# The preparation of a pair of RWKV heads as three workers: front, values, back

## The chip, the cores and the metric

The kernel runs on one core of a Trainium2 chip. The metric is the device time of one execution in microseconds (us). The profile tells of five engines, each with its own queue of instructions: TensorE (PE, with its weight loads as PEld), VectorE (DVE), ScalarE (ACT), GpSimd (POOL) and SyncE (SP, which here only issues DMAs).

## What is computed

One decoder layer on 512 tokens of width 2048, in float32: a forgetting-attention branch (fox, 8 heads of 128) and an RWKV-7 branch (16 heads of 64), each with a gate, are projected, gated by sigmoids, added, multiplied by `w_out`, added to the input and normalized. Cut to the RWKV branch, which the change concerns:

```python
h = _rmsnorm(x, norm_gain)
u = h @ w_in
...
r, kr, vr, z_b, w_down, a_down = _split(_token_shift(u_rwkv, mix), RWKV_SIZES)
w = -softplus(-(w0 + tanh(w_down) @ w2)) - 0.5
decay = exp(-exp(w));  a = sigmoid(a0 + a_down @ a2)
kk = heads(kr * k_k) / norm;  kr = kr * (1 + (a - 1) * k_a)
for t in tokens:                      # per head, S is 64 x 64
    sa = S @ (-kk[t])
    S = S * decay[t] + outer(sa, (kk * a)[t]) + outer(v[t], kr[t])
    y[t] = S @ r[t]
o_b = (groupnorm(y) * ln_w + ln_b + bonus) * silu(z_b)
```

## The kernel before, in words

**Tiles of the big products.** The input is normalized and transposed once (`hhi`, `hlo`: a high and a low part, so that each float32 product is three matmuls of 512 columns). A *tile* `u_<name>` is 128 output columns of `w_in`: 16 blocks of the contraction by three matmuls, 48 in all. Its weights come in four *pieces* of 256 KB: `load_raw` (L237) issues a load on SP into one of `RAWS` buffers, ScalarE makes the high part `whi` (L262), VectorE the low part `wlo` (L263). `next_piece` (L240) issues loads `RAWS` pieces ahead and emits the two splits three pieces ahead of use.

**Order of the tiles.** `units` (L295) lists them: pair 0, pair 1, then a fox head and a pair by turns, at last fox head 6. A pair of RWKV heads has four tiles in the order k, r, z, v; a fox head has q, k, v, z. After them (`stage1`, L859 on) come the merge tiles `u_g` (three of them, then fox head 7, then one g tile and one projection `p` by turns) and the output product `o`. The first `p` needs the results of all eight pairs, loaded back from memory (`oraw`, L870).

**Workers and the planner's clock.** The order of TensorE's and of SP's instructions is the order in which the program emits them (`manual_schedule`, L152); VectorE, ScalarE and GpSimd are ordered by the framework from the program order and priorities. The small steps are generators (*workers*) that yield a lag. `clock` advances with each matmul by its planned cost (`mm`, L125: 512/2370 us for one of a tile); after each matmul of a tile `drive` (L112) runs every worker whose lag has passed, first worker in the list first. So a lag says how much TensorE work is put between two steps. The lags stand in `LAG` (L51).

**A pair's preparation before** (`rwkv_prep`, L489), a single worker that starts when the one of the pair before is done (`after=[prep, chain2]`, L851):
- front: the small `lora` weights are loaded and split (L498 to L502), the square of k is split; after a lag of 3.57 (`in`) the products `kn`, `lw` and `la` (eight matmuls); from them on VectorE, ScalarE and GpSimd the decay (scan, exponentials E1 and E2), `kp`, the normalized `kk` (reciprocals, L535), `AR` (L540, L541), `BK` (four products on 64 partitions, L546 and L549), `rkk` and its split `rhi`, `rlo`;
- values: after 11.25 (`vt0`), and when the v tile is there (`vin`), transposes of v (`vt`), the bonus (`bn`, L574), centring of `SV`, copies to `AV` (L586, on GpSimd);
- back: after 9.77 (`sc0`) the scores `sc` (two halves of 16 recorded matmuls each, 8.02 apart) from `BK` and `AR`, masked into `G`; `G` goes through memory and comes back as `Lt` (L609, L613); the solve, 31 steps of a product and a reduction on VectorE (L618 to L621); 42 after its emission the result goes through memory again (L626 to L634); after 5.04 (`inv`), and when the chain before is done, `bt`, `gp` and `dp`.

**The chain** (`rwkv_chain`, L673) runs the state over eight chunks (`z`, `sa`, `st`), then `y`, the group norm and the store to `ob_d`. Chain and preparation of different pairs overlap. **Fox heads** (`fox_head`, L751) are workers too, last in the list.

Buffers that the change touches: `EK` holds E2 and `kp` and later `Lt`; `W` and `Wt` hold `lora` and `lora_l` and later the solve; four tags (`t0`, `a`, `t2`, `EK`) are used again by the first merge tiles, which is why `stage1` waits for `free["rw"] == 7` (L859), set when the solve of the last pair is emitted (L622).

Of the kernel before, what the change touches and what calls it, by code (L numbers as in the profile page):

```python
# [9 lines left out]
F32 = mybir.dt.float32  # L10
F32R = mybir.dt.float32r
# [12 lines left out]
CH = 64  # L24
NC = T // CH
LORA = 96
# [19 lines left out]
AHEAD = 8  # L46
SQ2 = 6
SQ3 = 14
RAWS = 5

LAG = {"in": 3.57, "vt0": 11.25, "vt": 1.47, "sc0": 9.77, "sc": 8.02, "bt": 1.78, "inv": 5.04, "sub": 42.0, "gp": 2.84, "ch": 1.31, "z": 1.2, "sa": 1.6, "st": 2.01, "gn": 3.3, "gv": 1.42, "f0": 4.37, "f1": 2.11, "f2": 11.56, "f3": 3.14, "f4": 4.67, "f5": 16.0, "f6": 1.12}  # L51


@with_exitstack
def hybrid_layer(
# [23 lines left out]
    clock = [0.0]  # L79

    class Worker:
        def __init__(self, gen, after):
            self.gen, self.after, self.ready, self.done = gen, after, clock[0], False

        def runnable(self):
            return not self.done and all(w is None or w.done for w in self.after)
# [6 lines left out]

    workers = []

    def spawn(gen, after=(), first=True):
        w = Worker(gen, after)
        workers.insert(0, w) if first else workers.append(w)
        return w

    def step_one(force=False):
# [19 lines left out]
    def until(cond):  # L121
        while not cond():
            yield "wait"
# [360 lines left out]
    hs = [slice(0, 64), slice(64, 128)]  # L484
    free = {}

    made, zs = {}, {}

    def rwkv_prep(p, r, k):  # L489
        def w(tag, shape=(P, T), n=None, bufs=1, dt=F32):  # L490
            return (keep if tag in KEEP else rw).tile(list(shape), dt, tag=tag, name=f"{n or tag}_{p}", bufs=bufs)

        def col(base):
            return par[:, base + p:base + p + 1]

        v = vT[:, CH:CH + T]
        E1, DT = E1s[p % 2], DTs[p % 2]
        lora = w("W", (LORA, 2, P), n="lora")  # L498
        nc.sync.dma_start(lora[:, 0, :], rwkv_w2[0][:, p * P:(p + 1) * P])
        nc.sync.dma_start(lora[:, 1, :], rwkv_a2[0][:, p * P:(p + 1) * P])  # L500
        lo2 = [w("lora", (LORA, 2, P), dt=F32R, n="lora_h"), w("Wt", (LORA, 2, P), dt=F32R, n="lora_l")]
        split(*lo2, lora)  # L502
        ksq = w("t2", n="ksq")
        S.activation(ksq, k, AF.Square, scale=col(R_KK))
# [34 lines left out]
        AR = w("AR", (P, NC, 2 * CH), bufs=2)  # L539
        V.scalar_tensor_tensor(AR[:, :, 0:CH], c3(kk), -1.0, E1[:, :, 0:CH], ALU.mult, ALU.mult)  # L540
        tt(V, AR[:, :, CH:], c3(r), E1[:, :, 1:CH + 1])  # L541
        BK = w("BK", (P, NC, 2 * CH))
        tt(G, kk, kk, a)
        for q in range(2):
            h = hs[q]
            tt(V, BK[h, :, 64 - 64 * q:128 - 64 * q], c3(kp)[h], c3(E2)[h])  # L546
        for q in range(2):
            h = hs[q]
            tt(V, BK[h, :, 64 * q:64 * q + 64], c3(kk)[h], c3(E2)[h])  # L549

        t2 = w("t2", n="rkk")
        V.scalar_tensor_tensor(t2, r, col(R_RK), kp, ALU.mult, ALU.mult)
        rhi, rlo = w("t0", n="rhi", dt=F32R), w("t3", n="rlo", dt=F32R)
        split(rhi, rlo, t2)
        free["rk"] = p
        yield LAG["vt0"]
        while free.get("vin", -1) < p:
            yield 1.0

        SV, AV = w("SV", (P, NC, 2, CH), bufs=2), w("AV", (P, NC, 2, CH), bufs=2)  # L560
        for w0 in (0, 4, 8):
            ps = ps_ms(f"vt_{p}_{w0}").rearrange("p (c t) -> p c t", c=4)
            n = min(4, 9 - w0)
# [16 lines left out]
        for q in range(2):  # L580
            h = hs[1 - q]
            vm = w(f"vm{q}", (P, NC))
            V.tensor_reduce(vm[h], SV[h, :, q, :], AX.X, ALU.add)
            V.scalar_tensor_tensor(SV[h, :, q, :], vm[h].unsqueeze(2).broadcast_to([64, NC, CH]), -1.0 / 64,
                                   SV[h, :, q, :], ALU.mult, ALU.add)
            G.tensor_copy(AV[h, :, q, :], SV[h, :, q, :])  # L586
            G.memset(SV[hs[q], 0, q, :], 0.0)
        yield LAG["sc0"]
        while free.get("chain", -1) < p - 2:
            yield 1.0  # L590

        Gm = w("G", (P, NC, 2, 2, CH), bufs=2)
        mask4 = smask.rearrange("p (k t) -> p k t", k=2)[:, None].broadcast_to([P, 4, 2, CH])
# [12 lines left out]
        for q in range(2):  # L606
            for b in range(2):
                o = 64 * q + 32 * b
                nc.sync.dma_start(l_d[16 * q + 8 * b:16 * q + 8 * b + 8].rearrange("c s t -> s c t"),  # L609
                                  Gm[o:o + 32, :, 0, q, 32 * b:32 * b + 32])  # L610
        Lt = w("EK", (P, 32, 32), n="Lt")
        for g in range(4):
            nc.sync.dma_start(Lt[32 * g:32 * g + 32], l_d)  # L613
        V.memset(Lt.rearrange("p s t -> p (s t)")[:, 0:1024:33], 1.0)
# [3 lines left out]
        for i in range(1, 32):  # L618
            tt(V, tmp[:, :, 0:i + 1], W[:, :, 0:i + 1],
               Lt[:, 0:i + 1, i].unsqueeze(1).broadcast_to([P, 8, i + 1]))  # L620
            V.tensor_reduce(W[:, :, i], tmp[:, :, 0:i + 1], AX.X, ALU.add)  # L621
        free["rw"] = p  # L622
        yield LAG["sub"]
        w_d = dram.tile([32, 4, 256], F32, tag="w_d", bufs=2, name=f"w_d_{p}")
        for g in range(4):
# [41 lines left out]
        for q in range(2):  # L667
            h = slice(64 * q, 64 * q + 32)
            (V.tensor_copy if q else S.copy)(DT[h, :, 64 * q + 32:64 * q + 64], dp[h, 0:NC, :])
            S.copy(Gm[hs[q], :, 0, q, :], AR[hs[q], :, 0:CH])  # L670
        made[p] = (AR, BT, DT, SV, AV, Gm, E1, bonus)

    def rwkv_chain(p):  # L673
        def w(tag, shape=(P, T), n=None, bufs=1, dt=F32):
            return (keep if tag in KEEP else rw).tile(list(shape), dt, tag=tag, name=f"{n or tag}_{p}", bufs=bufs)

        def col(base):
            return par[:, base + p:base + p + 1]

        AR, BT, DT, SV, AV, Gm, E1, bonus = made.pop(p)  # L680
        yield LAG["ch"]


        for c in range(NC):
            with tc.high_priority(offset=HP):
                zp = ps_ch(f"z_{p}_{c}")
                mm(zp, Gm[:, c, 0].rearrange("p q t -> p (q t)"), SV[:, c])
                zt = w("zt", (P, CH), bufs=2)
                V.tensor_copy(zt[hs[0]], zp[hs[0], 0, :])
                S.copy(zt[hs[1]], zp[hs[1], 1, :])  # L690
                pre = w("pre", (P, CH))
                if c < NC - 1:
                    for q in range(2):
                        S.activation(pre[hs[q]], SV[hs[q], c, q, :], AF.Copy, scale=E1[hs[q], c, CH:CH + 1])
            yield LAG["z"]
            with tc.high_priority(offset=HP):
                sa = ps_ch(f"sa_{p}_{c}")
                mm(sa[:, 0, :], DT[:, c, :], zt)
                V.tensor_copy(AV[hs[0], c, 0, :], sa[hs[0], 0, :])
                S.copy(AV[hs[1], c, 1, :], sa[hs[1], 0, :])  # L700
            yield LAG["sa"]
            if c < NC - 1:
                with tc.high_priority(offset=HP):
                    st = ps_ch(f"st_{p}_{c}")
                    mm(st, BT[:, c, :], AV[:, c])
                    for q in range(2):
                        V.scalar_tensor_tensor(SV[hs[q], c + 1, q, :], st[hs[q], q, :], E1[hs[q], c, CH:CH + 1],
                                               pre[hs[q]], ALU.mult, ALU.add)
                yield LAG["st"]

        y = psm.tile([P, NC, CH], F32, tag="y", bufs=1, name=f"y_{p}")
        for c in range(NC):
            for q in range(2):
                mm(y[hs[q], c, :], SV[hs[q], c, q, :], AR[hs[q], c, CH:], start=(c == 0), stop=False,
                   skip_group_check=True)
        for c in range(NC):
            for q in range(2):
                mm(y[hs[q], c, :], AV[:, c, q, :], Gm[:, c, 1, q, :], start=False, stop=(c == NC - 1),
                   skip_group_check=True)
        yield LAG["st"]  # L720
        free["chain"] = p

        z = zs.pop(p)
        with tc.high_priority(offset=HV):
            yf = y.rearrange("p c t -> p (c t)")
            ysq = ps_ms(f"ysq_{p}")
            S.activation(ysq, yf, AF.Square)
            yhi, ylo = w("y", n="yhi", dt=F32R), w("y2", n="ylo", dt=F32R)
# [82 lines left out]
    def fox_unit(i):  # L811
# [13 lines left out]
        def run(i=i, ins=ins):  # L825
            yield from fox_head(i, ins)
            free["fox"] = i
        spawn(run(), first=False)

    def stage1():  # L830
        ps = yield from u_tile("ad")
        ad = keep.tile([LORA, T], F32, tag="t2", name="ad")
        shift(ad, ps, R_MUA, LORA)
        split(*ads, ad)
        prep = chain = chain2 = None
        ins = {}
        for kind, i in units:
            if kind == "rw":
                for nm, blk in (("k", 1), ("r", 0), ("z", 3), ("v", 2)):
# [8 lines left out]
                        ins[nm] = dst  # L848
                    shift(dst, ps, R_MU + blk * 8 + i)
                    if nm == "r":  # L850
                        prep = spawn(rwkv_prep(i, ins["r"], ins["k"]), after=[prep, chain2])  # L851
                        chain2 = chain
                        chain = spawn(rwkv_chain(i), after=[prep, chain])
                    if nm == "z":
                        zs[i] = dst
                free["vin"] = i
            else:
                yield from fox_unit(i)
        yield from until(lambda: free.get("rw", -1) == 7)  # L859


        mg_stack = ExitStack()
# [172 lines left out]
```

## Time and profile before

| | |
|---|---|
| median of 3 runs | 1706.83 us (1701.46 to 1707.15) |
| the profiled execution | 1702.85 us |
| its span, first to last instruction | 1701.1 us, mean granted clock 0.991 |
| TensorE matmul busy | 1640.5 us (96%), 8506 instructions |
| VectorE busy | 962.1 us (57%) |
| ScalarE busy | 716.9 us (42%) |
| GpSimd busy | 91.1 us (5%) |
| chain that ended last | 85% TensorE, 9% VectorE, 2% ScalarE, 1% DMA |

Matmuls are pipelined: the recorded duration of one (0.39 us for 512 columns) is longer than the distance of their starts (10.88 us for 48, that is 0.227), so a short wait can hide in the busy time, and distances of starts tell more than durations. Engines are named as in the profile, and L133 is line 133 of the kernel. A float32 product of small tiles is recorded as two instructions.

### The profile page before, as it was taken

To read this page: it belongs to the slowest core of one execution; us is meant where nothing else is said; L and a number is where in the kernel's file an instruction comes from. 1 tells how busy PE (TensorE), PEld (TensorE's weight loads), DVE (VectorE), ACT (ScalarE), POOL (GpSimd) and SP (SyncE) were. 2 spreads that over 40 slices of the span, in tenths; PEclk is the share of its full clock that TensorE was granted. 3 is DMA by queue.
4 is the path that set the end of the run, shared out by engine and by line. 5 is a ranking of instruction groups with operands and counts; after the bars stand their busy time and mean duration, and the time that the engine had idled before them with its cause. 6 is when DMAs were issued, how large, how long until landed. Compare 5 with 4: busy or idle time off the path is not lost.

```text
span 1701.1 us, 23407 instructions
## 1 busy us (share of the span) xinstructions
PE 1640.5 (96%) x8506; PEld 1332.3 (78%) x8506; DVE 962.1 (57%) x2005; ACT 716.9 (42%) x1455; POOL 91.1 (5%) x149
## 2 busy tenths in 40 slices
PE   6999999999999999999999988999999999999998
PEld 6878778788787787787877876888888888888886
DVE  6657577876786677867877644223233333353432
ACT  7522653654635536555355344222223222243322
POOL 3000000100001001000010000000000000001110
PEclk9999999999999999999999998999999999999999
DMA  5334234333333333333333324335334333343422
GB/s 170 84 90 107 71 100 105 77 97 97 82 91 84 83 97 83 97 85 90 88 90 90 96 63 130 99 95 147 95 97 145 97 96 97 98 141 137 133 81 99
DMA packets 287977, 170.23 MB, mean 100 GB/s; under 512 B 38790, under 2 KB 270830, under 8 KB 287222
## 3 DMA queue, kind: packets, MB, share of 16 engines
q1 hardware_dynamic: 284358, 156.13, 34.5%
q0 software_dynamic: 2064, 9.46, 1.6%
q10 hardware_dynamic: 1440, 3.15, 0.5%
q8 instruction: 67, 1.10, 0.3%
q14 instruction: 48, 0.39, 0.1%
HBM read 158.19 MB, written 10.50 MB: 99 GB/s over the span
## 4 chain that ended last, share of the span: by engine, by line
PE 85%; DVE 9%; ACT 2%; DMA 1%; issue 1%; SPq 1%; ACTq 0%; POOL 0%; DVEq 0%
PE u_g L133 21%; PE o L133 10%; PE p L133 10%; PE u_fk L133 5%; PE u_fq L133 5%; PE u_v L133 5%; PE u_z L133 5%; PE u_r L133 5%; PE u_fv L133 4%; PE u_fz L133 3%; PE u_k L133 3%; DVE BK L478 2%; DVE kn L535 1%; PE fo L133 1%; PE y L133 1%
## 5 line engine op out<-in xcount | busy, mean ns | idle before, releaser
L133 PE MATMUL u_g<-hhi,whi_g 128*128 128x512 f32 x512 | 200.7, 392 | 0.0
L133 PE MATMUL u_g<-hhi,wlo_g 128*128 128x512 f32 x512 | 200.5, 392 | 0.0
L133 PE MATMUL u_g<-hlo,whi_g 128*128 128x512 f32 x512 | 199.8, 390 | 0.0
L263 DVE TENSOR_TENSOR wlo_g<-raw_g,whi_g 128x512 fp32r<-128x512 f32 x128 | 88.5, 692 | 170.7 <-ACT whi_g L262 163.1
L262 ACT ACTIVATE whi_g<-raw_g 128x512 fp32r<-128x512 f32 x128 | 80.7, 632 | 223.6 <-PE u_g L133 120.6
L133 PEld LDWEIGHTS u_g<-hhi,wlo_g 128*128 128x128 f32 x512 | 96.3, 188 | 20.4
L133 PEld LDWEIGHTS u_g<-hlo,whi_g 128*128 128x128 f32 x512 | 96.3, 188 | 20.2
L133 PE MATMUL p<-ohi,whi_p 128*128 128x512 f32 x256 | 102.2, 399 | 10.1 <-ACT ohi L874 10.1
L133 PEld LDWEIGHTS u_g<-hhi,whi_g 128*128 128x128 f32 x512 | 96.2, 188 | 20.0
L263 DVE TENSOR_TENSOR wlo_p<-raw_p,whi_p 128x512 fp32r<-128x512 f32 x64 | 44.3, 692 | 108.2 <-ACT whi_p L262 108.2
L478 DVE TENSOR_TENSOR Wt<-W,Lt 128x16 f32<-128x16 f32 (+30 forms) x248 | 101.4, 409 | 5.9
L133 PE MATMUL p<-olo,whi_p 128*128 128x512 f32 x256 | 101.0, 394 | 0.2 <-DVE olo L876 0.2
L133 PE MATMUL p<-ohi,wlo_p 128*128 128x512 f32 x256 | 101.1, 395 | 0.0
L262 ACT ACTIVATE whi_p<-raw_p 128x512 fp32r<-128x512 f32 x64 | 40.5, 632 | 121.2 <-PE u_g L133 119.5
L133 PE MATMUL o<-whi_o,mhi 128*128 128x512 f32 x224 | 87.3, 390 | 0.1
L133 PE MATMUL o<-whi_o,mlo 128*128 128x512 f32 x224 | 87.2, 389 | 0.0
L133 PE MATMUL o<-wlo_o,mhi 128*128 128x512 f32 x224 | 87.2, 389 | 0.0
L263 DVE TENSOR_TENSOR wlo_o<-raw_o,whi_o 128x512 fp32r<-128x512 f32 x56 | 42.6, 761 | 77.3 <-ACT whi_o L262 77.1
L621 DVE TENSOR_REDUCE W<-Wt 128x8 f32<-128x16 f32 (+30 forms) x248 | 72.6, 293 | 5.8
L262 ACT ACTIVATE whi_o<-raw_o 128x512 fp32r<-128x512 f32 x56 | 35.3, 631 | 84.8 <-PE o L133 79.8
L133 PEld LDWEIGHTS p<-ohi,whi_p 128*128 128x128 f32 x256 | 48.6, 190 | 21.1 <-ACT ohi L874 11.2
L133 PE MATMUL u_fz<-hhi,wlo_fz 128*128 128x512 f32 x128 | 53.5, 418 | 7.1 <-DVE wlo_fz L263 7.0
(352 smaller groups left out, 3932.2 us busy)
## 6 DMA issues: line engine op xcount, KB each, us to landing
raw_g<-in_w_in_dram SPq DMA_DIRECT2D x128, 256.0 KB
raw_o<-in_w_out_dram SPq DMA_DIRECT2D x56, 256.0 KB
raw_k<-in_w_in_dram SPq DMA_DIRECT2D x32, 256.0 KB
raw_r<-in_w_in_dram SPq DMA_DIRECT2D x32, 256.0 KB
raw_z<-in_w_in_dram SPq DMA_DIRECT2D x32, 256.0 KB
raw_v<-in_w_in_dram SPq DMA_DIRECT2D x32, 256.0 KB
raw_fq<-in_w_in_dram SPq DMA_DIRECT2D x32, 256.0 KB
raw_fk<-in_w_in_dram SPq DMA_DIRECT2D x32, 256.0 KB
```

Source lines behind the costliest of these rows:

```text
L133: PE.matmul(out, lhsT=lhsT, rhs=rhs, start=start, stop=stop, **kw)
L262: S.activation(whi, raw, AF.Copy)
L263: (G if j < 4 else V).tensor_tensor(wlo, raw, whi.bitcast(F32), ALU.subtract)
L478: eng.tensor_tensor(o, a, b, op)
L535: V.reciprocal(t3[:, sl], t3[:, sl])
L621: V.tensor_reduce(W[:, :, i], tmp[:, :, 0:i + 1], AX.X, ALU.add)
```

## The change

`rwkv_prep` is cut into three workers. `rwkv_front` goes from the lora loads to the split of `rkk`; it starts when the front before it and chain p-2 are done, and waits until `BK` and the values of the pair before are emitted. `rwkv_values` starts after its front. `rwkv_back` starts after its front and the back before it; its first step is `BK`. The chain waits for back, values and the chain before. The list of workers is now ordered by rank: chain 0, back 1, front and values 2, fox heads 9. The lag before the scores is 5.0 in place of 9.77 and counts from `BK`. `lora`, its two parts and `Lt` get tiles of their own, `rlo` moves from `t3` to `a`, `AV` has one buffer in place of two and is filled at the start of the chain, and there are four buffers for raw weights in place of five. `stage1` goes on to the merge when `BK` of pair 7 is emitted.

```diff
-RAWS = 5
+RAWS = 4
-LAG = {... "sc0": 9.77, ...}
+LAG = {... "sc0": 5.0, ...}
...
-    def spawn(gen, after=(), first=True):
-        w = Worker(gen, after)
-        workers.insert(0, w) if first else workers.append(w)
+    def spawn(gen, after=(), rank=9):
+        w = Worker(gen, after, rank)
+        workers.append(w)
+        workers.sort(key=lambda w: w.rank)
         return w
...
-    def rwkv_prep(p, r, k):
+    def rwkv_front(p, r, k):
...
-        v = vT[:, CH:CH + T]
-        E1, DT = E1s[p % 2], DTs[p % 2]
-        lora = w("W", (LORA, 2, P), n="lora")
+        E1 = E1s[p % 2]
+        while free.get("bk", -1) < p - 1 or free.get("v", -1) < p - 1:
+            yield 1.0
+        lora = w("lora", (LORA, 2, P))
...
-        lo2 = [w("lora", (LORA, 2, P), dt=F32R, n="lora_h"), w("Wt", (LORA, 2, P), dt=F32R, n="lora_l")]
+        lo2 = [w("lora_h", (LORA, 2, P), dt=F32R), w("lora_l", (LORA, 2, P), dt=F32R)]
...
-        BK = w("BK", (P, NC, 2 * CH))
         tt(G, kk, kk, a)
-        for q in range(2):
-            h = hs[q]
-            tt(V, BK[h, :, 64 - 64 * q:128 - 64 * q], c3(kp)[h], c3(E2)[h])
-        for q in range(2):
-            h = hs[q]
-            tt(V, BK[h, :, 64 * q:64 * q + 64], c3(kk)[h], c3(E2)[h])
 
         t2 = w("t2", n="rkk")
         V.scalar_tensor_tensor(t2, r, col(R_RK), kp, ALU.mult, ALU.mult)
-        rhi, rlo = w("t0", n="rhi", dt=F32R), w("t3", n="rlo", dt=F32R)
+        rhi, rlo = w("t0", n="rhi", dt=F32R), w("a", n="rlo", dt=F32R)
         split(rhi, rlo, t2)
         free["rk"] = p
+        made[p] = (AR, kk, kp, E2, E1)
+        sums[p] = (rhi, rlo)
+
+    def rwkv_values(p):
...
+        rhi, rlo = sums.pop(p)
         yield LAG["vt0"]
         while free.get("vin", -1) < p:
             yield 1.0
...
-            G.tensor_copy(AV[h, :, q, :], SV[h, :, q, :])
             G.memset(SV[hs[q], 0, q, :], 0.0)
+        vals[p] = (SV, bonus)
+
+    def rwkv_back(p):
...
+        AR, kka, kp, E2, E1 = made.pop(p)
+        DT = DTs[p % 2]
+        BK = w("BK", (P, NC, 2 * CH))
+        for q in range(2):
+            h = hs[q]
+            tt(V, BK[h, :, 64 - 64 * q:128 - 64 * q], c3(kp)[h], c3(E2)[h])
+        for q in range(2):
+            h = hs[q]
+            tt(V, BK[h, :, 64 * q:64 * q + 64], c3(kka)[h], c3(E2)[h])
+        free["bk"] = p
         yield LAG["sc0"]
-        while free.get("chain", -1) < p - 2:
-            yield 1.0
...
-        Lt = w("EK", (P, 32, 32), n="Lt")
+        Lt = w("Lt", (P, 32, 32))
...
-        free["rw"] = p
...
     def rwkv_chain(p):
...
+        SV, bonus = vals.pop(p)
+        AV = w("AV", (P, NC, 2, CH))
+        for q in range(2):
+            h = hs[1 - q]
+            G.tensor_copy(AV[h, :, q, :], SV[h, :, q, :])
         yield LAG["ch"]
...
-                        prep = spawn(rwkv_prep(i, ins["r"], ins["k"]), after=[prep, chain2])
+                        front = spawn(rwkv_front(i, ins["r"], ins["k"]), after=[front, chain2], rank=2)
+                        values = spawn(rwkv_values(i), after=[front], rank=2)
+                        back = spawn(rwkv_back(i), after=[front, back], rank=1)
                         chain2 = chain
-                        chain = spawn(rwkv_chain(i), after=[prep, chain])
+                        chain = spawn(rwkv_chain(i), after=[back, values, chain], rank=0)
...
-        yield from until(lambda: free.get("rw", -1) == 7)
+        yield from until(lambda: free.get("bk", -1) == 7)
```

## Rows read from the trace of the kernel before

**Rows 1.** The page, busy tenths in 40 slices of the span, TensorE.

```profile
PE   6999999999999999999999988999999999999998
```

**Rows 2.** Busy time by stretch: from:to, length, engines' busy us, clock, DMA, GB/s.

```profile
core 0: us, PE busy (x) PEld busy (x) DVE busy (x) ACT busy (x) POOL busy (x), PEclk, DMA share, GB/s
84.00:95.00 11.00, 8.56 (x31) 6.59 (x30) 7.27 (x11) 2.52 (x4) 0.83 (x3) 0.84 0.47 119
...
320.00:332.00 12.00, 9.06 (x43) 6.89 (x42) 11.64 (x29) 7.29 (x22) 1.98 (x2) 1.00 0.30 79
540.00:552.00 12.00, 8.96 (x32) 7.15 (x33) 8.99 (x18) 3.89 (x10) 0.61 (x1) 0.72 0.40 109
...
895.00:910.00 15.00, 11.73 (x129) 9.53 (x128) 7.97 (x26) 6.53 (x21) 0.00 (x0) 0.89 0.17 42
1014.00:1041.00 27.00, 15.18 (x50) 9.91 (x50) 17.73 (x31) 15.16 (x28) 0.54 (x1) 0.75 0.46 136
1041.00:1500.00 459.00, 459.00 (x2012) 376.94 (x2011) 146.02 (x218) 126.64 (x216) 1.63 (x3) 1.00 0.39 106
```

**Rows 3.** Waits of TensorE: us in total, times, longest us.

```profile
PE p L133 <- ACT ohi L874: 10.1, 2, 9.9
...
PE u_fz L133 <- DVE wlo_fz L263: 7.0, 3, 3.7
...
PE u_k L133 <- DVE wlo_k L263: 6.3, 3, 3.0
```

**Rows 4.** Chain that ended last, in order of time: start us, us, what.

```profile
57.98 10.88 PE u_r L133 x48
...
124.73 10.89 PE u_z L133 x48
...
234.30 2.10 PE u_z L133 x9
...
366.06 10.88 PE u_v L133 x48
...
478.99 10.88 PE u_v L133 x48
...
814.59 10.88 PE u_z L133 x48
```

**Rows 5.** Timeline of TensorE, pair 3, and the first chain product of pair 7.

```profile
415.74 0.39 PE L133 MATMUL kn<-khi,bones 128*128 128x512 f32 x1
...
428.55 0.60 PE L137 MATMUL vt<-ident,vT 128*128 128x128 f32 x4
...
446.16 1.16 PE L133 MATMUL sc<-AR,BK 64*128 64x128 f32 x16
...
520.39 0.69 PE L133 MATMUL dp<-DT,GP 32*32 32x32 f32 x32
...
968.95 0.38 PE L133 MATMUL z<-SV,G 128*128 128x128 f32 x2
```

**Rows 6.** Timeline of TensorE, pair 0: the front's products and the matmul after them.

```profile
72.78 0.40 PE L133 MATMUL kn<-khi,bones 128*128 128x512 f32 x1
...
74.63 0.40 PE L133 MATMUL u_z<-hhi,whi_z 128*128 128x512 f32 x1
```

**Rows 7.** Timeline of VectorE: the last two products of BK, pairs 0 and 3.

```profile
85.07 1.38 DVE L478 TENSOR_TENSOR BK<-kn,EK 64x512 f32<-64x512 f32 x2
...
429.91 1.39 DVE L478 TENSOR_TENSOR BK<-kn,EK 64x512 f32<-64x512 f32 x2
```

**Rows 8.** Waits of SP's queue: us in total, times, longest us.

```profile
SPq L870 <- DVE y L745: 12.7, 1, 12.7
```

**Rows 9.** Timelines of SP and ScalarE: a weight load and its conversion, twice.

```profile
1102.90 0.37 SPq L237 DMA_DIRECT2D raw_g<-in_w_in_dram  x1
...
1115.23 0.63 ACT L262 ACTIVATE whi_g<-raw_g 128x512 fp32r<-128x512 f32 x1 [2.09 <-PE u_g L133]
...
1558.15 0.33 SPq L237 DMA_DIRECT2D raw_l<-in_w_out_dram  x1
...
1560.76 0.62 ACT L971 CAST lhi<-raw_l 128x512 fp32r<-128x512 f32 x1 [0.64 <-DMA raw_l<-in_w_out_dram]
```

More of the change, by code (lines that the diff above doesn't have):

```diff
@@ L48 @@
 SQ3 = 14
-RAWS = 5
-LAG = {"in": 3.57, "vt0": 11.25, "vt": 1.47, "sc0": 9.77, "sc": 8.02, "bt": 1.78, "inv": 5.04, "sub": 42.0, "gp": 2.84, "ch": 1.31, "z": 1.2, "sa": 1.6, "st": 2.01, "gn": 3.3, "gv": 1.42, "f0": 4.37, "f1": 2.11, "f2": 11.56, "f3": 3.14, "f4": 4.67, "f5": 16.0, "f6": 1.12}
+RAWS = 4
+LAG = {"in": 3.57, "vt0": 11.25, "vt": 1.47, "sc0": 5.0, "sc": 8.02, "bt": 1.78, "inv": 5.04, "sub": 42.0, "gp": 2.84, "ch": 1.31, "z": 1.2, "sa": 1.6, "st": 2.01, "gn": 3.3, "gv": 1.42, "f0": 4.37, "f1": 2.11, "f2": 11.56, "f3": 3.14, "f4": 4.67, "f5": 16.0, "f6": 1.12}
 @with_exitstack
@@ L81, in hybrid_layer, with __init__ @@
     class Worker:
-        def __init__(self, gen, after):
-            self.gen, self.after, self.ready, self.done = gen, after, clock[0], False
+        def __init__(self, gen, after, rank):
+            self.gen, self.after, self.ready, self.done, self.rank = gen, after, clock[0], False, rank
         def runnable(self):
@@ L485, in hybrid_layer @@
     free = {}
-    made, zs = {}, {}
-    def rwkv_prep(p, r, k):
+    made, sums, vals, zs = {}, {}, {}, {}
+    def rwkv_front(p, r, k):
         def w(tag, shape=(P, T), n=None, bufs=1, dt=F32):
@@ L541, in rwkv_prep, with w @@
         tt(V, AR[:, :, CH:], c3(r), E1[:, :, 1:CH + 1])
-        BK = w("BK", (P, NC, 2 * CH))
         tt(G, kk, kk, a)
-        for q in range(2):
-            h = hs[q]
-            tt(V, BK[h, :, 64 - 64 * q:128 - 64 * q], c3(kp)[h], c3(E2)[h])
-        for q in range(2):
-            h = hs[q]
-            tt(V, BK[h, :, 64 * q:64 * q + 64], c3(kk)[h], c3(E2)[h])
         t2 = w("t2", n="rkk")
         V.scalar_tensor_tensor(t2, r, col(R_RK), kp, ALU.mult, ALU.mult)
-        rhi, rlo = w("t0", n="rhi", dt=F32R), w("t3", n="rlo", dt=F32R)
+        rhi, rlo = w("t0", n="rhi", dt=F32R), w("a", n="rlo", dt=F32R)
         split(rhi, rlo, t2)
         free["rk"] = p
+        made[p] = (AR, kk, kp, E2, E1)
+        sums[p] = (rhi, rlo)
+    def rwkv_values(p):
+        def w(tag, shape=(P, T), n=None, bufs=1, dt=F32):
+            return (keep if tag in KEEP else rw).tile(list(shape), dt, tag=tag, name=f"{n or tag}_{p}", bufs=bufs)
+        v = vT[:, CH:CH + T]
+        rhi, rlo = sums.pop(p)
         yield LAG["vt0"]
@@ L558, in rwkv_prep @@
             yield 1.0
-        SV, AV = w("SV", (P, NC, 2, CH), bufs=2), w("AV", (P, NC, 2, CH), bufs=2)
+        SV = w("SV", (P, NC, 2, CH), bufs=2)
         for w0 in (0, 4, 8):
@@ L585, in rwkv_prep, with w @@
                                    SV[h, :, q, :], ALU.mult, ALU.add)
-            G.tensor_copy(AV[h, :, q, :], SV[h, :, q, :])
             G.memset(SV[hs[q], 0, q, :], 0.0)
+        vals[p] = (SV, bonus)
+    def rwkv_back(p):
+        def w(tag, shape=(P, T), n=None, bufs=1, dt=F32):
+            return (keep if tag in KEEP else rw).tile(list(shape), dt, tag=tag, name=f"{n or tag}_{p}", bufs=bufs)
+        AR, kka, kp, E2, E1 = made.pop(p)
[8 more added lines that the diff above has]
+        free["bk"] = p
         yield LAG["sc0"]
-        while free.get("chain", -1) < p - 2:
-            yield 1.0
         Gm = w("G", (P, NC, 2, 2, CH), bufs=2)
@@ L670, in rwkv_prep @@
             S.copy(Gm[hs[q], :, 0, q, :], AR[hs[q], :, 0:CH])
-        made[p] = (AR, BT, DT, SV, AV, Gm, E1, bonus)
+        made[p] = (AR, BT, DT, Gm, E1)
     def rwkv_chain(p):
@@ L678, in col @@
             return par[:, base + p:base + p + 1]
-        AR, BT, DT, SV, AV, Gm, E1, bonus = made.pop(p)
+        AR, BT, DT, Gm, E1 = made.pop(p)
+        SV, bonus = vals.pop(p)
[3 more added lines that the diff above has]
+            G.tensor_copy(AV[h, :, q, :], SV[h, :, q, :])
         yield LAG["ch"]
@@ L827, in run @@
             free["fox"] = i
-        spawn(run(), first=False)
+        spawn(run())
     def stage1():
@@ L834, in stage1 @@
         split(*ads, ad)
-        prep = chain = chain2 = None
+        front = back = chain = chain2 = None
         ins = {}
```

## Prediction

> **What bounds the kernel now.** I read the busy shares first, then the busy time by stage, then the chain of waits in order of time, then TensorE's and VectorE's own timelines round single pairs, and last the waits of SP. TensorE is full in nearly every fortieth of the span [rows 1], and from 1041 to 1500 us it is busy all of the 459 us at a granted clock of 1.00 [rows 2]: that second part (merge and output product) can't be shortened by moving work, and the change doesn't touch its arithmetic. So the question is what TensorE waits for before 1041 us, and the change can win only what it waits there. The rows show three kinds of waiting. (a) The end of the pair stage: from 895 to 910 us TensorE is busy 11.7 of 15.0 us at clock 0.89, and from 1014 to 1041 us it is busy 15.2 of 27.0 us at 0.75 [rows 2]. There the stream of tiles has run out and the last pair's solve and chain are emitted with nothing beside them; the first projection `p` waits 9.9 us of this for its operand [rows 3]. (b) Waits of 2.4 to 3.7 us for split weights that VectorE delivers late (`u_fz` 7.0 us in 3 waits, `u_k` 6.3 us in 3 [rows 3], and the 2.4 us of idle at pair 0 between 84 and 95 us [rows 2]). (c) Sub-microsecond waits inside the chain, which stay.
>
> **Where a pair stands against the tiles.** A tile of 48 matmuls takes 10.88 us, and from the v tile of one pair to that of the next are 112.9 us (366.06 to 478.99) [rows 4]. Before, the preparation of pair 3 trails its tiles far: its v tile, two tiles behind its r tile, already starts at 366.06 us [rows 4], its `kn` product at 415.74 [rows 5]. That is so because preparations run one after the other: from the scores `sc` at 446.16 to `dp` at 520.39 alone are 75 us [rows 5], and front and values come before that.
>
> In the changed kernel only the back is serial: BK (four products, about 4 us on VectorE; two of them took 1.39 [rows 7]), a planned 5.0, then these 75 us, some 84 us in all. 84 is less than 113. So the preparation catches up with the tiles and then waits for them: a front can't start before its r tile. Pair by pair: pair 0 starts its front right after its r tile (57.98 + 10.88 = 68.9; `kn` at 72.78) [rows 4, 6], as before. Its back ends near 87 + 75 = 162. The r tile of pair 1 ends at 124.7 [rows 4], so front 1 does run under solve 0, 33 us ahead of its back. Back 1 ends near 162 + 84 = 246; the r tile of pair 2 ends before 234.3 [rows 4], and front 2's `kn` comes some 4 us after it: ahead of its back by a few us only. Back 2 then ends near 246 + 84 = 330, the r tile of pair 3 some 18 us later (366.06 less one tile of 10.88 and the work between [rows 4], with the few us that the waits below add). From pair 3 on, back p-1 is done before front p begins: 113 us lie between two r tiles, and front and back take about 90. **So for pairs 0 and 3 to 7 the front isn't under a neighbour's solve: the back follows its own front at once.**
>
> **What this costs: the scores are placed too early.** `rwkv_front` emits its products and all of its VectorE work in one step; the back is runnable in the same loop and emits BK with no lag, and the scores 5.0 planner units later. Planner units are close to us here: `vt` with its lag of 11.25 came 12.8 us after `kn` (415.74 to 428.55), of which the eight products of the front are 1.85 (72.78 to 74.63) [rows 5, 6]. So `sc` stands on TensorE's queue 1.85 + 5.0 to 5.3, some 7.0 us behind `kn`. TensorE's order is fixed, so all tiles behind `sc` wait with it, and the chain of the pair before too. BK is ready much later: its last two products end at 86.45 for pair 0, 13.7 us after `kn`, and at 431.30 for pair 3, 15.6 us after [rows 5 to 7]; VectorE works through the front until then. Before, `sc` came 30 us after `kn` [rows 5] and never met this. The first score product needs the first and third of the four writes, so I take off half of the last row's 1.39: it can start 13.0 and 14.9 us after `kn`. **Wait: 6.0 us for pair 0, 7.9 for pairs 3 to 7, together 45 us.** Lower end: 6.0 for all six, 36. Upper end: the fourth write is awaited (6.7 and 8.6), and pair 2 is late too: 58.
>
> After such a wait the clock is low. The waits at 84 and 540 us are followed by a mean of 0.84 over 11 us and 0.72 over 12 us [rows 2], that is 1.8 and 3.4 us lost, while between 320 and 332 us TensorE idled 2.9 us and kept 1.00 [rows 2]. The new waits are two to three times as long as these, so I take 1.8 for each of six, 10.8 (0 to 3.4 each). The Trainium skill (TensorE: Matmul & The Clock Gate, "HAM oscillation") says that an array that waits again in every tile is throttled again each time; by that rule the term stands at its 10.8, while the wait after 320 us disagrees with it. By the share of the three short waits shown here, two of which cost clock, the term would be 7.
>
> **What it removes.** (a) Chain 7 starts some 20 us of front and 84 of back after its r tile, near 920 (its z tile starts at 814.6 [rows 4]) in place of 969 [rows 5], and ends about 50 us earlier, under tiles; the loads of `oraw`, which stood 12.7 us on SP behind pair 7's last result [rows 8], find their memory free. The two stretches lose 3.3 + 1.6 and 11.8 + about 3.8 us (idle, and the low clock on working time) [rows 2]: 20.5 us. Next late is the work that fills them, the same tiles, which run at full rate. Lower end 12, if the eight `oraw` loads still pace the first projection. (b) The late splits came from the same burst of VectorE work; where TensorE now stands at `sc`, the splits catch up meanwhile. `u_fz`'s 7.0, pair 0's 2.4, some 0.3 of `u_k` and the clock after them (1.8 + 3.4) go: 14.9 us. The two `u_k` waits near 3 us belong to pairs 1 and 2 and stay.
>
> **What costs nothing.** Instruction counts are the same. Four weight buffers instead of five: with five, a load is issued 12.3 us before its conversion starts (1102.90 to the fifth conversion on at 1115.23) and pieces come every 2.72 us, so four leave 9.6; a load converted as soon as it had landed took 2.6 us (1558.15 to 1560.76) [rows 9]. Where the output stage loads three pieces for every two that it multiplies, 9.6 shrinks to some 6, still above 2.6. If the cover were gone each pair would lose about one piece, 2.7 us. The lora loads have their own tile and no longer make SP wait for the pair before; the weight loads behind them come sooner. The 18 loads and stores of a pair's solve keep their order. The two AV copies move on POOL from the values to the start of the chain, some 5 us ahead of the first `st` that reads them; behind them POOL has the next front's two products, which come tens of us later.
>
> **Sum.** 45 + 10.8 - 20.5 - 14.9 = +20.4 us. The profiled execution took 1702.85 (span 1701.1), 4.0 under the median of the runs, 1706.83; carried to the median, 1727.2. Low end of this case 36 + 0 - 20.5 - 14.9 = +1, 1707; high end 58 + 7 x 3.4 - 20.5 - 14.9 = +46, 1753.
>
> **Rivals.**
> 1. *Faster: BK is in time, as the description has it.* If the r tiles were emitted well before the backs are done, or VectorE did BK first, `sc` would find its operand. Then only the end is won: -20.5, 1686; with (b) too, 1672. It decides where `sc` starts less than 2 us late. For it: pair 1 certainly runs so, and pair 2 nearly. Against: 84 against 113 us. Chance 0.17.
> 2. *No difference.* The waits stay at the low end, the clock holds, the small chain waits shrink because the fronts no longer fall on a chain's beginning: +1, 1708, from -8 to +8. Chance 0.19.
> 3. *Slower by weight loads.* SP stands at the score store until the masks are done, and with `sc` late it stands there longer; with one buffer fewer the next pieces could be late as well, 2.7 us for each of eight pairs: 1727 + 22 = 1749. The 9.6 against 2.6 us speak against it. Chance 0.07, within the slower side.
>
> **How the numbers follow.** The forecast has 0.57, rival 3 has 0.07, rival 2 has 0.19, rival 1 has 0.17. A measurement can tell about 0.5% (8.5 us) from no change: slower 0.64, same 0.19, faster 0.17. The forecast's own range is 1707 to 1753; the range given takes in rival 2 and the edge of rival 1, 1694 to 1755.
>
> **What would show it.** Right: `sc` of pairs 0 and 3 to 7 begins with 6 to 9 us idle put down to BK; none at pair 1; `kn` about 4 us behind the r tile from pair 3 on; the stretch between the last `u_fz` and the first `p` full; no 10 us wait at `p`; second part unchanged. Wrong: `sc` starts without a wait at pair 4 or 5, or `kn` of pair 5 still tens of us behind its r tile, or waits for raw weights.

## The result, and the profile after

The changed kernel takes 1755.93 us (median of 4 runs, 1755.21 to 1756.53) against 1704.88 us beside it: a ratio of 1.0301, 95% interval 1.028 to 1.0322. It is slower by 51 us. The forecast had 20 us slower, with a range that ended at 1755. The profiled execution has a span of 1753.5 us, 52.4 more than before, at a mean granted clock of 0.978 (before 0.991).

TensorE's tenths of the page now show slices at 8 over the whole pair stage (one at 7), and the clock is below nine tenths in three of them; in [rows 1] only the end dipped:

```profile
PE   6898989998989989989979999999999999999998
...
PEclk9999999998999989989999999999999999999999
```

By stretch (the columns are those of [rows 2]): the start of pair 0; the scores of pair 3; the end of the pair stage; the second part up to 1550 us.

```profile
84.00:95.00 11.00, 8.58 (x35) 7.01 (x36) 6.97 (x10) 1.44 (x4) 0.66 (x3) 0.61 0.25 66
...
390.00:412.00 22.00, 14.01 (x122) 12.02 (x121) 16.29 (x26) 10.16 (x20) 3.77 (x2) 0.77 0.10 24
...
895.00:1083.00 188.00, 176.97 (x994) 144.08 (x993) 108.56 (x236) 77.70 (x167) 7.61 (x8) 0.98 0.36 94
1084.00:1550.00 466.00, 466.00 (x2047) 382.70 (x2046) 153.33 (x234) 132.26 (x228) 1.63 (x3) 1.00 0.40 107
```

The second part is as full as it was. The end of the pair stage, which lost 15 us of idle in two stretches before, idles 11 us in all of 895 to 1083, most of it one wait of pair 7's scores. What is new lies where the scores are. TensorE's waits (total, times, longest), against [rows 3] (`yv` is the group norm's product behind a chain, `lw` one of the front's):

```profile
PE sc L134 <- DVE BK L479: 44.8, 8, 8.0
PE vt L138 <- DVE vT L445: 8.9, 6, 2.6
...
PE sa L134 <- ACT zt L711: 7.3, 18, 1.2
PE u_v L134 <- DVE wlo_v L264: 5.4, 1, 5.4
...
PE yv L134 <- DVE ylo L423: 5.0, 5, 1.4
PE lw L134 <- ACT lora_h L422: 2.7, 1, 2.7
```

The scores wait 44.8 us for BK; the waits of `p` (10.1 in [rows 3]), `u_fz` and `u_k` are gone. Pair 4 in TensorE's timeline shows the mechanism; it answers to pair 3 of [rows 5]. The bracket is the idle time ahead of the instruction and what ended it:

```profile
512.11 0.40 PE L134 MATMUL kn<-khi,bones 128*128 128x512 f32 x1
...
520.97 0.39 PE L134 MATMUL z<-SV,G 128*128 128x128 f32 x2
527.74 2.58 PE L134 MATMUL sc<-AR,BK 64*128 64x128 f32 x15 [6.38 <-DVE BK L479]
```

And VectorE's timeline of the same stretch, which answers to [rows 7]:

```profile
514.97 1.76 DVE L537 RECIPROCAL kn<-kn 128x128 f32<-128x128 f32 x2
...
522.77 0.74 DVE L547 SCALAR_TENSOR_TENSOR rkk<-r,par,EK 128x512 f32<-128x512 f32 x1
...
524.03 2.35 DVE L479 TENSOR_TENSOR BK<-EK 64x512 f32<-64x512 f32 x2
526.40 0.69 DVE L423 TENSOR_TENSOR rlo<-rkk,rhi 128x512 fp32r<-128x512 f32 x1
527.01 1.40 DVE L479 TENSOR_TENSOR BK<-kn,EK 64x512 f32<-64x512 f32 x2
```

`kn` comes 4.0 us behind the end of the r tile (508.1), TensorE is at the scores 9 us later, and BK is ready 16 us after `kn`, because VectorE does the whole front first. Lastly the stretches of the pair stage in which the granted clock was half (1.2 of 2.4 GHz), all nine of them. The second number is the length, the third TensorE's busy time in it:

```profile
82.30:92.60 10.30, 6.18 (x24) 5.09 (x25) 7.50 (x11) 1.46 (x4) 1.72 (x3) 0.50 0.19 51
150.60:157.40 6.80, 6.10 (x14) 4.78 (x15) 4.49 (x8) 0.78 (x2) 1.56 (x1) 0.50 0.52 135
259.80:266.60 6.80, 5.90 (x46) 4.60 (x45) 5.08 (x9) 5.46 (x11) 1.21 (x1) 0.50 0.00 0
399.80:410.00 10.20, 5.60 (x66) 5.04 (x68) 7.79 (x11) 0.62 (x1) 1.55 (x1) 0.50 0.11 26
526.10:532.90 6.80, 5.16 (x23) 4.23 (x24) 5.06 (x9) 0.21 (x1) 0.00 (x0) 0.50 0.15 39
645.50:655.80 10.30, 5.18 (x23) 4.35 (x24) 8.97 (x14) 1.31 (x3) 1.55 (x1) 0.50 0.18 51
771.80:782.10 10.30, 7.05 (x28) 5.83 (x29) 6.87 (x11) 0.94 (x3) 0.65 (x1) 0.50 0.10 26
806.00:809.40 3.40, 3.40 (x11) 2.81 (x12) 3.19 (x11) 0.68 (x2) 0.26 (x2) 0.50 0.66 196
901.50:908.40 6.90, 4.39 (x21) 3.75 (x22) 5.93 (x9) 0.16 (x1) 0.61 (x1) 0.51 0.16 40
sum 71.80, PE 48.97 PEld 40.47 DVE 54.89 ACT 11.60 POOL 9.11; mean PE 5.44 PEld 4.50 DVE 6.10 ACT 1.29 POOL 1.01
```

If work at half clock takes twice its time, half of the 48.97 us was lost to the clock, 24.5 us. The kernel before had four such stretches with 18.6 us of work in them, 9.3 us lost; their sum:

```profile
sum 27.30, PE 18.58 PEld 14.37 DVE 15.68 ACT 8.88 POOL 0.54; mean PE 4.64 PEld 3.59 DVE 3.92 ACT 2.22 POOL 0.13
```

(Idle time in a slow stretch costs nothing by the clock, so the mean clock would overstate it.) Half is an estimate on the high side: the matmuls of a tile start 0.43 us apart in these stretches and 0.23 outside, and over the fourteen traces of this case TensorE's busy time grows by 0.41 us (0.32 to 0.50) for each us of work at half clock.

**The balance.** TensorE's idle time is span less busy time: 1701.1 - 1640.5 = 60.6 before, 1753.5 - 1651.3 = 102.2 after, so 41.6 us of the 52.4 are idle and 10.8 are busy. The idle part by the lists of waits: `sc` +44.8; `vt` +8.6 (8.9, and 1.4 for `Lt`, less 1.7); `u_v` and `u_r` +4.2; `yv` +3.0; `lw` +2.7; `sa` +2.3; `dp` +1.2; against `p` -10.3, `u_fz` -7.0, `u_k` -6.3, `z` -1.8. Together +41.4. The busy part is the clock, +15.2, less some 4 us. Most of the 4 is probably the estimate itself: by 0.41 in place of a half the clock comes to +12.3, and the 1.5 us left are within the scatter of those traces (some 2 us).

### The profile page after: what moved, and what is told of

Read it like the earlier page. It is cut to its first block, busy times and chain, and to the rows that moved or that the text cites. A ratio compares the mean times of both kernels' runs of the same rounds, so it can differ in the third digit from the quotient of the medians.

```text
span 1753.5 us, 23443 instructions
## 1 busy us (share of the span) xinstructions
PE 1651.3 (94%) x8506; PEld 1345.7 (77%) x8506; DVE 964.4 (55%) x2005; ACT 714.2 (41%) x1455; POOL 86.7 (5%) x149
## 4 chain that ended last, share of the span: by engine, by line
PE 82%; DVE 11%; ACT 4%; issue 2%; DMA 1%; SPq 0%; DVEq 0%; ACTq 0%
PE u_g L134 20%; PE p L134 10%; PE o L134 10%; PE u_v L134 5%; PE u_fv L134 4%; PE u_fz L134 4%; PE u_fk L134 4%; PE u_r L134 4%; PE u_k L134 4%; PE u_fq L134 4%; PE u_z L134 3%; DVE Wt L479 2%; PE sc L134 1%; DVE W L638 1%; DVE kn L537 1%
## 5 line engine op out<-in xcount | busy, mean ns | idle before, releaser
L134 PEld LDWEIGHTS u_g<-hhi,whi_g 128*128 128x128 f32 x512 | 96.2, 188 | 19.6
L134 PE MATMUL sc<-AR,BK 64*128 64x128 f32 x256 | 29.2, 346 | 44.8 <-DVE BK L479 44.8
L134 PEld LDWEIGHTS sc<-AR,BK 64*128 64x128 f32 x256 | 23.9, 238 | 50.2 <-DVE BK L479 41.2
```

The source lines that it names most:

```text
L134: PE.matmul(out, lhsT=lhsT, rhs=rhs, start=start, stop=stop, **kw)
```

## The experiments

All of them compute the same as the kernel. "Idle" is span less busy time of TensorE in the profiled execution; "half" its busy time at half clock in the pair stage, by the unrounded edges of the stretches.

| run | edit | median us | ratio to before | idle | half |
|---|---|---|---|---|---|
| before | | 1704.88 | | 60.6 | 18.6 |
| after | the change | 1755.93 | 1.0301 [1.028, 1.0322] | 102.2 | 48.8 |
| e1 | after, score lag 14.0 | 1714.07 | 1.0056 [1.0037, 1.0074] | 74.6 | 17.0 |
| e2 | after, score lag 9.77 | 1718.18 | 1.0082 [1.0064, 1.01] | 75.8 | 31.3 |
| e9 | after, v transposes 2.5 later | 1745.09 | 1.0237 [1.022, 1.0254] | 94.2 | 45.2 |
| e4 | e1 and e9 together | 1705.31 | 1.0007 [0.9996, 1.0019] | 64.7 | 22.7 |
| e5 | e4, weight splits first | 1706.35 | 1.0011 [1.0001, 1.0022] | 66.7 | 23.6 |
| e10 | e4, front after the solve | 1705.88 | 1.0003 [0.9993, 1.0013] | 66.3 | 10.2 |
| e11 | e4, front after the back | 1705.62 | 1.0007 [0.9998, 1.0016] | 64.3 | 14.7 |
| e3 | before, four weight buffers | 1710.03 | 1.0027 [1.0015, 1.0039] | 64.7 | 24.5 |
| e6 | before, weight splits first | 1715.55 | 1.006 [1.0045, 1.0075] | 64.2 | 35.8 |
| e12 | before, score lag 5.0 | 1697.05 | 0.9958 [0.9945, 0.9972] | 55.5 | 18.2 |
| e13 | before, lags 9.0 and 7.0 | 1702.97 | 0.9988 [0.9979, 0.9997] | 58.3 | 17.0 |
| e14 | e12, late v transposes 4.0 later | 1695.06 | 0.9949 [0.9934, 0.9965] | 56.5 | 19.6 |

**e1 and e2: the score lag alone.**

```diff
-LAG = {... "sc0": 5.0, ...}
+LAG = {... "sc0": 14.0, ...}     (e2: 9.77, the number of before)
```

> The changed kernel with the lag before the scores raised from 5.0 to 14.0. Theory A (the scores stand on TensorE's queue before BK is done): the 44.8 us of waits of sc on BK fall below 5 us, the time at half clock before the merge falls from 71 us to below 35 us, and the kernel takes 1756 - 45 - 15 to 22 = 1689 to 1696 us, faster than the kernel before. Theory B (four weight buffers are what costs): the waits at sc go, but late weights take their place; 1740 us or more. Theory C (the waits at sc stand in for the late splits, which return when they go): sc waits gone, 15 us of waits of tiles for their low parts come back, about 1705 us.

> The changed kernel with the lag of the kernel before, 9.77, counted from BK. Theory A: sc stands 4.8 us of planned work later, so each of the seven waits of 6 to 8 us shrinks by about 5 us to 1 to 3 us, 44.8 us to about 12 us; the waits are then as short as those that did not always cost clock, so half-clock time falls to 25 to 45 us; 1756 - 33 - 12 = about 1711 us. Theory B: 1745 us or more. Theory C: about 1720 us.

Measured: 14.0 gives back 41.9 us of the 51, the old 9.77 gives back 37.8. Both come out slower than theories A and C had them. TensorE's waits of e1, from the top of its list: no row for `sc` is left, but other rows have grown.

```profile
PE u_v L134 <- DVE wlo_v L264: 13.8, 3, 6.1
PE vt L138 <- DVE vT L445: 11.6, 7, 1.9
PE sa L134 <- ACT zt L711: 10.5, 16, 1.4
...
PE yv L134 <- DVE ylo L423: 6.9, 8, 1.4
PE u_r L134 <- DVE wlo_r L264: 5.6, 1, 5.6
```

The cause of the waits at the scores is shown: move the scores back and they go. But of the 44.8 us of waiting only 27.6 are gone from the idle time (102.2 to 74.6): the other 17 come back as waits of `u_v`, `u_r`, `vt`, `sa` and `yv` for results of VectorE and ScalarE. (The clock's part falls from 24.4 to 8.5 us.) Two of the three `u_v` waits (3.1 and 4.6 us) are in pairs 0 and 3, whose v tile came behind a long wait at the scores in the changed kernel. The likely reason is that VectorE had caught up with the splits while TensorE stood there, and now it doesn't. With 9.77 one wait of 3.6 us for BK is left.

**e9 and e4: the transposes of v.** In the changed kernel `vt` starts 1.7 to 2.1 us behind the end of its v tile in seven of eight pairs (3.7 in pair 6), after a wait for a VectorE result: its operand `vT` in six pairs, in the other two the profile names `Lt` (in [rows 5] the values trailed their tile by tens of us).

```diff
         while free.get("vin", -1) < p:
             yield 1.0
+        yield 2.5
```

> The changed kernel with its lag of 5.0 and only the transposes of v 2.5 planned us later. Theory A: the waits of sc on BK stay at 40 to 45 us in seven places, those of vt (8.9 + 1.4 us) fall below 2; 1756 - 8 to 10 = 1746 to 1748 us. If the waits only pass to the next product, 1753 us or more.

> As the run with lag 14.0, and the values wait 2.5 planned us more once the v tile is emitted, before the transposes. If the transposes of v stand on the queue before the shift of v is done (8.9 us of waits in 6 places in the changed kernel), these waits fall below 2 us and the kernel gains 6 to 9 us on the run with lag 14.0 alone. If they are only another face of VectorE being full, the wait moves to the next product and the gain is below 3 us.

Measured: 10.8 us from this line alone, 8.8 on top of e1, and no `vt` row is left in either. So the two lags give back all of the 51 us: e4 stands at the time of before. It doesn't stand below it, although the first `p` waits for nothing in e4 (9.9 us in [rows 3]): its two longest waits are

```profile
PE u_v L134 <- DVE wlo_v L264: 13.7, 3, 6.1
PE sa L134 <- ACT zt L712: 11.1, 16, 1.4
```

The 6.1 us one is pair 1, the one pair whose front really lies under the solve of its neighbour. VectorE's timeline there: between these two splits of one tile lie 17.3 us, in which it does steps of solve 0 (`Wt`) by turns with the front (the scan).

```profile
127.38 0.68 DVE L264 TENSOR_TENSOR wlo_v<-raw_v,whi_v 128x512 fp32r<-128x512 f32 x1
...
135.22 1.22 DVE L518 TENSOR_TENSOR_SCAN tz<-reset,tz 128x512 f32<-128x512 bf16 x1
136.35 0.48 DVE L479 TENSOR_TENSOR Wt<-W,Lt 128x176 f32<-128x176 f32 x1
...
144.72 0.68 DVE L264 TENSOR_TENSOR wlo_v<-raw_v,whi_v 128x512 fp32r<-128x512 f32 x1
```

**e5 and e6: VectorE does weight splits first.** The same edit in e4 and in the kernel before:

```diff
+            with tc.high_priority(offset=100 if j >= 8 else 0):
                 ... (the two instructions that split a piece)
```

> The run with lag 14.0 and the later transposes, and the splits of the weights get a higher priority in the framework's order of ScalarE and VectorE (offset 100), so that a front or a solve no longer comes ahead of them. Theory A with C (with the scores in place, what is left are splits that a burst of VectorE work holds back: u_v 13.7, u_r 5.6 and u_fk 3.7 us of waits and the clock after them): these 23 us fall below 6 and the kernel takes 1705 - 17 to 25 = 1680 to 1688 us. Rival (the remaining loss is not in the splits but in the chain's and the group norm's own waits, which splits put first would lengthen): 1700 to 1712 us.

> The kernel before with the same higher priority for the splits of the weights and nothing else. Theory A with C: u_fz 7.0, u_k 6.3 and u_v 2.4 us of waits go, with some 5 us of clock; the 10 us wait at p stays; 1705 - 13 to 20 = 1685 to 1692 us. Rival: the splits delay the chain instead, 1700 us or more.

Measured: no gain in e5 (+1 us), a loss of 11 us in e6. The wait goes to whatever the splits now overtake. In e5 `u_z` waits 6.8 us in one piece for the shifted k, `fvt` 6.2 and `u_fq` 5.3. In e6 it is the bonus product, which waits for the split of `rkk`, while the wait at `p` stays:

```profile
PE bn L133 <- ACT rhi L422: 12.5, 7, 3.4
PE p L133 <- ACT ohi L875: 10.1, 2, 9.9
```

**e3: four buffers in the kernel before.**

```diff
-RAWS = 5
+RAWS = 4
```

> The kernel before with four buffers for raw weights in place of five and nothing else. Theory A: no difference, within 4 us of the kernel before. Theory B: slower by 20 us or more, with TensorE waiting for splits whose ScalarE half waited for a load.

Measured: +4.5 us. Two new rows appear in TensorE's waits between 900 and 1045 us, beside the one of `p`:

```profile
PE p L133 <- ACT ohi L874: 9.9, 1, 9.9
...
PE u_g L133 <- ACT whi_g L262: 1.6, 1, 1.6
...
PE u_g L133 <- DVE wlo_g L263: 1.2, 1, 1.2
```

Both are at one place (927 us, a merge tile), and it isn't the load that is late: the four pieces were issued by 913, and from 917 to 929 us the DMA engines move nothing (the last two numbers), so they had landed. ScalarE converts the first of them only at 926.3, behind other work; with five buffers its first conversion of a g piece there comes at 914.1.

```profile
917.00:929.00 12.00, 9.18 (x42) 6.90 (x41) 11.66 (x40) 8.75 (x19) 0.59 (x1) 1.00 0.00 0
...
926.27 1.15 ACT L262 ACTIVATE whi_g<-raw_g 128x512 fp32r<-128x512 f32 x2
```

So four buffers cost through the order of work on ScalarE, and why that order differs is open. In the changed kernel no such row stands, so how much of its 51 us this is can't be read; five buffers beside its new tiles were not tried.

**e10 and e11: no front under the solve.** If the fronts under a neighbour's solve cost e4 its gain, moving them should bring it out. In e10 the front waits until the result of the solve of the pair before is sent to memory (42 behind its emission), in e11 until its whole back is.

```diff
-        while free.get("bk", -1) < p - 1 or free.get("v", -1) < p - 1:
+        while free.get("sol", -1) < p - 1 or free.get("v", -1) < p - 1:
...
         yield LAG["sub"]
+        free["sol"] = p          (e11: at the end of rwkv_back instead)
```

> The run with lag 14.0 and the later transposes, and a front may start only when the solve of the pair before has been sent to memory, so that no front runs under a solve. Only pairs 1 and perhaps 2 are moved. Theory A with C (a front among the 62 solve steps keeps the splits off VectorE longest: 17 us between two splits at pair 1): the wait of 6.3 us of u_v at pair 1 falls to 0 to 3.5 us, as in the kernel before; 1705 - 3 to 6 = 1699 to 1702 us. Rival (overlapping a front with a solve is worth something, as the description has it): 1706 us or more.

> The kernel of the run e10 with one thing changed: front p waits until the whole back of pair p-1 is emitted (its last product dp), in place of its solve. So no front stands beside a solve or a back any more; what is left of the change is the score lag of 14.0, the 2.5 units before the transposes of v, the earlier merge, and four weight buffers. My theory: in e10 the end of the pair stage is full (the first p at 1031 without a wait, some 20 us better than before), and all of it is given back in pairs 1 to 3, where a front still meets a neighbour's back: 25 us more start-to-start loss from 150 to 400 us than in the kernel before (a lora wait of 5.1 us in pair 2, z and sa waits of 2.1 and 3.3 us in pair 3, split weights 3.1 us twice). With the fronts behind the backs these go, the pairs run as before, and the end is still full: 1685 to 1692 us. Rival one: the loss doesn't depend on where the fronts of pairs 1 to 3 lie and comes back as split waits and sa waits in the next stretch, and the chain of pair 7 ends some 20 us later: 1700 to 1708, as e10. Rival two: the later chain 7 makes the first p wait again and the merge gate is late too: 1706 or more, with a wait of several us at p.

Measured: 1705.88 and 1705.62, as e4. That fells my theory for e11. Its first rival has the time and the waits for splits right; but pair 7's chain ends 6 us later than in e10, not 20. In e10 the 6 us wait of pair 1 is gone and others stand in its place, the first of these rows for a load of pair 2 that now stands behind the solve's on SP; in e11 five different tiles wait for a split.

```profile
PE lw L134 <- ACT lora_h L422: 5.1, 1, 5.1
...
PE u_z L134 <- DVE wlo_z L264: 2.9, 1, 2.9
```

```profile
PE u_r L134 <- DVE wlo_r L264: 5.7, 1, 5.7
PE u_fk L134 <- DVE wlo_fk L264: 5.1, 2, 3.0
PE u_fz L134 <- DVE wlo_fz L264: 4.3, 1, 4.3
```

**e12 to e14: the end alone, in the kernel before.** The end was late because each preparation waits for the one before, some 111 us apart from pair 1 on, while the r tiles of pairs 0 and 1 end only 56 us apart: `kn` stands 67 us behind its r tile in pair 1 and still 49 in pair 7. One number shortens that without new workers, since there the scores stand some 30 us behind `kn` and BK is ready after 16.

```diff
-LAG = {... "sc0": 9.77, ...}
+LAG = {... "sc0": 5.0, ...}      (e12; e13: "vt0" 9.0 and "sc0" 7.0)
```

> The kernel before with one number of the change alone: the lag ahead of the scores 5.0 in place of 9.77; one worker per pair, five weight buffers, the old gate. Here the scores still stand behind the values, some 26 us behind kn instead of 30, and BK ends 14 to 16 us behind kn, so I expect no wait of sc on BK. The preparations follow each other, so that each pair gains up to 4.8 us on its tiles, and the chain of pair 7 comes up to some 30 us earlier. Theory one: the wait of 9.9 us at the first projection and the low clock behind it are a loss of the end alone; they go, with the mean of the pair stage unchanged: 1685 to 1693 us. Theory two, from the runs e4, e10 and e11, which all have a full end and all come out at 1705 to 1706: what the end gives back is lost again as split waits and sa waits of the earlier pairs, because VectorE gets the same work for chains and preparations in a shorter stretch: 1702 to 1708. The two differ in the lost start-to-start time before 900 us: 102 us as in the kernel before by theory one, some 120 by theory two.

> The kernel before with the lag ahead of the values' transposes 9.0 in place of 11.25 and the lag ahead of the scores 7.0 in place of 9.77: the same 5 us per pair as in e12, taken at two places. By theory one 1685 to 1693, by theory two 1702 to 1708; if only the place matters (the transposes meet vT late, as in the changed kernel), it is slower than e12 by the waits of vt, at most 2 to 3 us for each pair.

Measured: e12 is 7.6 us faster than before, e13 1.7. In e12 pair 7's chain starts at 947.2 (968.95 in [rows 5]) and `p` waits no more. Neither theory held: of the 13 us that TensorE lost ahead of `p` (10.3 of waits and half of the 6.3 us of work at half clock behind it), somewhat more than half is kept. The rest comes back as the wait that the changed kernel also had, since the values now reach the v tile. It is the top row of e12's waits, and e13, which moves the transposes forward, has more of it:

```profile
PE vt L137 <- DVE vT L444: 9.7, 4, 4.7
```

```profile
PE vt L137 <- DVE vT L444: 11.7, 4, 6.9
```

e14 takes it away, where the v tile was waited for:

```diff
+        late = free.get("vin", -1) < p
         while free.get("vin", -1) < p:
             yield 1.0
+        if late:
+            yield 4.0
```

> The kernel of e12 (before with the score lag 5.0) and 4.0 planner units more ahead of the transposes of v, in those pairs alone whose v tile was waited for. In e12 the pairs 0, 5, 6 and 7 come up to their v tile and vt waits 9.7 us in 4 for vT, 4.7 of it in pair 5, where the clock is at half rate for 6.8 us behind it. I expect these waits nearly gone and 6 to 11 us won on 1697: 1686 to 1691. Rival: the transposes a little later push the scores and so the last chain later, and VectorE's backlog comes out at another place: 1694 to 1699.

Measured: 1695.06, 0.5% under the kernel before and the lowest of all, 2 us under e12 where I had put 6 to 11. Against the kernel before beside it that is 8.5 us, e12's was 7.6, and the two intervals overlap: what this edit adds isn't clear of the noise. No `vt` wait is left in e14; new ones for splits stand in its list, the longest of them

```profile
PE u_fk L133 <- DVE wlo_fk L263: 5.7, 2, 4.0
```

## Why the prediction was right, and where it failed

The direction and the largest term were right. Two steps failed: the term of the clock was taken too small, and what the rearrangement does besides the scores was put at nothing.

**Where a pair stands against the tiles: right.** From pair 3 on, the back before is emitted before the front begins (`dp` of pair 2 at 350.9, `kn` of pair 3 at 388.7), and `kn` comes about 4 us behind its r tile. Pair 1's front (`kn` at 133.9) lies under solve 0; pair 2's (254.9) is ahead of `dp` of pair 1 (261.6) by 7. So for six of eight pairs the overlap that the change is made for doesn't take place.

**The waits of the scores: right, in place and in size.** 45 us forecast, 44.8 measured. By pair, from the distance of starts: 6.4 at pair 0 (6.0 forecast), none at pair 1, 6.6 to 8.2 at pairs 3 to 7 (7.9); pair 2, forecast without a wait, has two that make 1.3.

**Removed, (a) and (b): mostly right as waits.** The end: 15.1 us of idle forecast to go, 12.1 went (`p` and `z`). Chain 7 starts 101 us ahead of the first `p` (982.9 against 1083.7), before 58. The `oraw` load's wait for pair 7's result [rows 8] has no row any more. The late splits: 9.7 of idle forecast, 9.1 went on balance (15.7 of `u_fz`, `u_k` and `u_v` became 6.6 of `u_v` and `u_r`). That these numbers are so near is in part luck: `u_k`'s 6 us, which I had left standing, went too, and 5.4 of `u_v` at pair 1 came new. The reason that I gave, that VectorE catches up while TensorE stands at the scores, fits e1: without the waits at the scores, `u_v` and `u_r` wait 19.4 us.

**The clock after the waits: the mechanism right, the term mis-sized.** I took 1.8 us for each of six waits from [rows 2], out of 0 to 3.4. The six stretches hold 33.6 us of work at half rate, 16.8 lost, 2.8 each: 6.0 too little. Three more stretches follow the waits of `u_v` (pair 1), `lw` (pair 2) and the transposes near 806 us, 7.7 lost, which I had not counted at all. So the clock cost 15.2 us net where my terms came to 0.2 (10.8 less the 5.4 in (a) and the 5.2 in (b); the 10.6 that these two make were 9.3 by working time). The rule of the Trainium skill (TensorE: Matmul & The Clock Gate, "HAM oscillation") that an array which waits again and again is throttled anew each time agrees here: at all six long waits the clock fell to half rate, for 6.8 to 10.3 us.

**"What costs nothing": the step that failed.** I named the BK wait as the one result that is late and costed the rest of the rearrangement at nothing: the values, the lora loads, the chain. They cost 17.8 us of idle: `vt` 8.6, since the values too catch up with their tile, by the very argument that I had made for the scores; `yv` 3.0, `lw` 2.7, `sa` 2.3, `dp` 1.2. e9 sizes the first with its clock at 10.8 us. The first is tested; the others are read from the lists of waits alone. The four weight buffers, also costed at nothing, cost 4.5 us in the kernel before (e3), but not by late loads, as rival 3 had it.

The sum then: 20.4 forecast; 17.8 and 15.0 (clock) missed, 3.6 of (a) and (b) not won, 4 of busy time the other way: 52.8, against 52.4 in the spans. **Rival 1** (the end won, 1672 to 1686) decided where the scores start in time. e1 and e4 put them there and come out at 1714 and 1705: even then the change isn't faster, and my rival was priced too well.

**What stays open.** e4, e5, e10 and e11 have a full end and differ in where fronts lie or which work VectorE does first, yet all take 1705 to 1706: some 13 us won at `p` are lost as waits of 2 to 6 us for VectorE at changing places. Shown is that these waits move when they are pushed (e1, e5, e10, e11, e14); that VectorE's order of work in the pair stage sets their sum was only argued, since no run made VectorE's work less. Nor was the new order of the workers tried by itself.

## What to carry to other kernels

When a serial stage is cut up so that its parts run earlier, ask for each part what it catches up with: every fixed distance that used to be covered by lateness (here the scores behind BK, the transposes behind `vT`) has to be set anew, and here each cost its wait and then the slow clock behind it. Before building workers, look for the number that holds the serial stage back: a lag 4.8 shorter won 0.4%, where three workers lost 3%. And a wait that is removed from an engine that runs in a fixed order can be worth less than its length, as its suppliers may have used it to catch up: here 44.8 us of waiting and 17 of clock were worth 42.

## What the runs showed of the hardware that was not expected

The same wait can keep or lose the clock. Pair 0's wait for a split of the v tile is as long in e4 as in e10 (3.25 us beyond the usual distance of starts, near 88 us), and TensorE is busy 7.91 of the 11 us round it in both; the granted clock (the sixth number behind the length) was 0.84 in e4 and 1.00 in e10:

```profile
84.00:95.00 11.00, 7.91 (x33) 5.82 (x33) 6.94 (x10) 1.64 (x3) 0.80 (x3) 0.84 0.47 119
```

```profile
84.00:95.00 11.00, 7.91 (x46) 6.03 (x45) 7.87 (x12) 1.90 (x3) 0.77 (x3) 1.00 0.46 120
```

These are one execution each; over the ten runs of e10 the mean granted clock was 0.990 to 0.996, over those of e4 0.989 to 0.993, so whether the kernel or the single execution decides is open. After the waits of 6 to 8 us at the changed kernel's scores it was lost each time, for 6.8 to 10.3 us. That is why I should not have carried the mean of short waits over to long ones.
